# A two-model fp32 block chain on one core: key projection in fp32, low-rank mixes folded into weights, triangular products and attention scores by alternating array halves, splits moved off POOL

## The chip, the cores and the metric

The kernel runs on one core of a Trainium2 chip. The time is device microseconds of one execution. Each engine has its own queue of instructions and runs it in order: PE (TensorE) does the matmuls, DVE (VectorE) and ACT (ScalarE) the elementwise work, POOL (GpSimd) takes some of it, SP (SyncE) starts most DMAs. PE's clock has two levels, 2.4 and 1.2 GHz; the profile gives the granted clock of a stretch as a share of the higher one.

## The reference

All data are float32, 256 positions of width 1024. The chain is RWKV-7 time mixing, a convolutional feed-forward block, sliding-window attention, another such block, then gMLP, MLP, forgetting attention, MLP. Three pieces are touched:

```python
# RWKV time mixing
xx = jnp.pad(x, ((0, 0), (1, 0), (0, 0)))[:, :-1] - x
xr, xw, xk, xv, xa, xg = [x + xx * mu[i] for i in range(6)]
r = xr @ w_rkv[0]; k = xk @ w_rkv[1]; v = xv @ w_rkv[2]
w = -jax.nn.softplus(-(w_decay0 + jnp.tanh(xw @ w_decay1) @ w_decay2)) - 0.5
a = jax.nn.sigmoid(a0 + (xa @ a1) @ a2)
g = jax.nn.sigmoid(xg @ g1) @ g2
def step(S, inp):               # per head, 64 x 64 state, over 256 positions
    r_t, d_t, k_t, v_t, a_t, b_t = inp
    sa = jnp.einsum('bhij,bhj->bhi', S, a_t)
    S = (S * d_t[:, :, None, :] + sa[..., None] * b_t[:, :, None, :]
         + v_t[..., None] * k_t[:, :, None, :])
    return S, jnp.einsum('bhij,bhj->bhi', S, r_t)
# forgetting attention, 16 heads of 64, blocks of 128 queries
logits = jnp.einsum('bhtd,bhsd->bhts', qb, kb) * scale + c_q - c_k   # causal
outs.append(jnp.einsum('bhts,bhsd->bhtd', softmax(logits), vb))
```

## The kernel before

**Weights.** A weight block of 128 x 2048 floats is a *unit*. `fetch` starts its DMA into a raw buffer; `split` turns it into a high part `hi` (a cast, L120, in four pieces, on ACT, some on DVE for units 0 and 1) and a remainder `lo` (raw minus hi, L122, four pieces, on DVE; a table gives some pieces of units 0, 1 and all of 10 to 13 to POOL). `mm3` (L146 to L148) then multiplies hi·hi, hi·lo and lo·hi in three matmuls of the one-pass type fp32r. Inputs of such a product are split the same way. A plain fp32 matmul needs no split; it stands in the trace as two matmul instructions, here called a *pair*.

**RWKV, first part.** For the low-rank branches w and a the kernel makes the mixed inputs x + xx·mu for each of 8 column blocks (`mixk`: one DVE operation L450, or ACT L447 and POOL L448), multiplies them by the 64-column weights (`pw` L474, `pa` L480), and then by the second factor (`pz` L498). For k, r and v `mixsplit` makes the mixed input and splits it (L450, then L138 on ACT and L139 on DVE). Each of the four units of k gives `pk` (48 fp32r matmuls of 128 x 256), its norm (`pn`, `pnb`) and the factors `AR`, `KB`; then come the four units of r (`pr`, L571, L573).

**Triangular products and inversion.** For four chunks c of 64 positions the products of KB and AR of every head go to `pm` (L605): ACT copies KB into a zero-padded tile `KZ` (L601), so that each product contracts over 128 rows of which 64 are zero. DVE masks the result (M, L606). A DVE transpose (L616) begins the inversion of 32 x 32 blocks: 31 steps j of one multiplication into `tm` (L623) and one addition into `TL` (L624), each needing the one before it, then two more transposes (L626, L627). Meanwhile PE runs the projections of v (`pv`), transposes (`pkt`), and the output gate (`pg` L660, L661, then `pgt` L674, L675).

**The chunk loop.** PE makes the blocks of the inverse (`pgm`, `pwm`), then for each chunk `pak`, `ry`, `pu`, `psn`, `py`, each with a copy on DVE or ACT before the next can start. POOL applies the gate (L809 to L813) and scales the state (L788). A group norm (`rv_gn`, L158 and on) and the output projection `wo` follow.

**Forgetting attention.** Scores `plf` (L1004) contract over the 64 rows of a head; heads with even numbers sit in the array's lower, odd ones in its upper 64 rows. Four heads of one half come before four of the other. The products with v (`pof`, L1045) write 64 of 128 output rows by the same rule. PE's queue is filled around them with projections (`fqk`, `fv`, `fg`).

A list scheduler sets each engine's order; the code's order and `tc.high_priority`, `tc.issue_after` steer it.

## Time and profile before

| | us |
|---|---|
| median of 3 runs (lowest, highest) | 1377.25 (1376.43, 1377.95) |
| the profiled execution | 1378.07 |
| its span, first to last instruction | 1376.4 |
| PE busy in the span | 1321.2 |
| DVE busy | 1071.2 |
| ACT busy | 840.4 |
| POOL busy | 129.3 |

An engine's busy time is the time in which one of its instructions runs. An engine idle in a stage that another one bounds costs nothing; so a stage is judged by the engine that is full in it.

### The profile page before, as it was taken

What the parts mean: (1) busy time and instruction counts of PE and PEld (TensorE: products, weight loads), DVE (VectorE), ACT (ScalarE), POOL (GpSimd) and SP (SyncE); (2) the same over time, 40 slices, a digit from 0 to 9 for tenths busy, and PEclk for the clock granted to TensorE, in tenths of its full rate; (3) what the DMA queues carried; (4) which work ended last, traced back from release to release, by engine and by line L of the source; (5) the groups of instructions that cost most, each with busy time, mean ns of one, the idle gap of its engine ahead of it and who ended that gap; (6) DMA issues with size and microseconds to landing.
All of it is one profiled execution on the core that took longest, in us unless ns stands there. A gap on an engine that the chain in (4) does not pass through costs nothing.

```text
span 1376.4 us, 21002 instructions
## 1 busy us (share of the span) xinstructions
PE 1321.2 (96%) x7776; PEld 1125.3 (82%) x7776; DVE 1071.2 (78%) x2296; ACT 840.4 (61%) x1793; POOL 129.3 (9%) x140
## 2 busy tenths in 40 slices
PE   6789888899999999999999999999999999999998
PEld 4788486688888977888888998888887788888887
DVE  8999968799888776998887986766668787576663
ACT  6675444677667874876667854655545766464551
POOL 3366380000000020000001000000000000000000
PEclk9999888999999999999999999999999999999999
DMA  5343202466553523565536554455553644265550
GB/s 212 125 152 111 74 2 92 154 233 226 185 193 128 184 92 107 199 235 202 202 131 225 200 193 158 172 212 191 199 189 118 254 155 151 78 229 192 197 192 31
DMA packets 35111, 226.30 MB, mean 164 GB/s; under 512 B 3744, under 2 KB 6208, under 8 KB 8896
## 3 DMA queue, kind: packets, MB, share of 16 engines
q1 hardware_dynamic: 32496, 215.69, 43.7%
q0 software_dynamic: 1760, 6.30, 1.4%
q10 hardware_dynamic: 752, 2.97, 0.6%
q8 instruction: 61, 1.00, 0.3%
q14 instruction: 42, 0.34, 0.1%
HBM read 223.87 MB, written 1.06 MB: 163 GB/s over the span
## 4 chain that ended last, share of the span: by engine, by line
PE 83%; DVE 12%; ACT 3%; issue 1%; DMA 1%; POOL 1%; DVEq 0%; ACTq 0%; SPq 0%
PE pu L299 9%; PE pm L299 7%; PE pu L297 6%; PE md L148 4%; PE md L146 4%; PE md L147 4%; PE pm L297 4%; PE fd L146 3%; PE fd L147 3%; PE fd L148 3%; DVE lo L122 1%; DVE TL L624 1%; DVE tm L623 1%; PE pu L295 1%; PE gu L148 1%
## 5 line engine op out<-in xcount | busy, mean ns | idle before, releaser
L122 DVE TENSOR_TENSOR lo<-raw,hi 128x512 fp32r<-128x512 f32 x680 | 441.6, 692 | 79.0 <-ACT hi L120 76.9
L120 ACT CAST hi<-raw 128x512 fp32r<-128x512 f32 x696 | 387.5, 618 | 142.8 <-PE md L148 52.3
L299 PE MATMUL pu<-X_n_x,hi 128*128 128x512 f32 x560 | 142.1, 393 | 0.0
L299 PEld LDWEIGHTS pu<-X_n_x,hi 128*128 128x128 f32 x560 | 100.1, 189 | 17.5
L299 PE MATMUL pm<-X_ml_x,hi 128*128 128x512 f32 x392 | 99.7, 393 | 0.0
L297 PEld LDWEIGHTS pu<-X_n_x,lo 128*128 128x128 f32 x640 | 87.4, 190 | 6.2
L297 PE MATMUL pu<-X_n_x,lo 128*128 128x256 f32 x640 | 89.7, 283 | 0.0
L299 PEld LDWEIGHTS pm<-X_ml_x,hi 128*128 128x128 f32 x392 | 70.0, 189 | 12.2
L117 DVE SCALAR_TENSOR_TENSOR lo<-raw,cv,hi 128x256 fp32r<-128x256 f32 (+1 forms) x136 | 67.3, 560 | 14.1 <-ACT hi L116 14.1
L116 ACT ACTIVATE hi<-raw,cv 128x256 fp32r<-128x256 f32 (+1 forms) x136 | 65.9, 560 | 14.5 <-DMA raw<-in_wst 8.9
L305 DVE TENSOR_TENSOR r<-pm,r 128x256 f32<-128x256 f32 x56 | 23.6, 424 | 57.3 <-ACT r L304 57.3
L304 ACT COPY r<-pm 128x256 f32<-128x256 f32 x56 | 20.8, 372 | 74.3 <-PE pm L299 74.3
L297 PEld LDWEIGHTS pm<-X_ml_x,lo 128*128 128x128 f32 x448 | 61.2, 190 | 4.3
L297 PE MATMUL pm<-X_ml_x,lo 128*128 128x256 f32 x448 | 62.7, 282 | 0.0
L939 ACT ACTIVATE ab<-zs,cv 128x256 f32<-128x256 f32 x80 | 47.5, 600 | 16.8 <-DVE zs L305 16.7
L147 PE MATMUL md<-lo,md0h 128*128 128x512 f32 x128 | 49.9, 390 | 0.0
L146 PE MATMUL md<-hi,md0h 128*128 128x512 f32 x128 | 49.8, 389 | 0.0
L148 PE MATMUL md<-hi,md0l 128*128 128x512 f32 x128 | 49.8, 389 | 0.0
L146 PE MATMUL md<-hi,md1h 128*128 128x512 f32 x128 | 49.8, 389 | 0.0
L147 PE MATMUL md<-lo,md1h 128*128 128x512 f32 x128 | 49.8, 389 | 0.0
L148 PE MATMUL md<-hi,md1l 128*128 128x512 f32 x128 | 49.8, 389 | 0.0
L940 DVE SCALAR_TENSOR_TENSOR ab<-zs,cv,ab 128x255 f32<-128x255 f32 x80 | 38.3, 481 | 10.7 <-ACT ab L939 9.2
(558 smaller groups left out, 3352.2 us busy)
## 6 DMA issues: line engine op xcount, KB each, us to landing
raw<-in_wst SPq DMA_DIRECT2D x200, 1024.0 KB, 4.8
g_n<-in_rows POOLq DMA_DIRECT2D x6, 512.0 KB, 4.5
ncb<-cd ACTq DMA_DIRECT2D x2, 1024.0 KB, 9.3
l2a<-in_lora SPq DMA_DIRECT2D x1, 1024.0 KB, 7.4
l2g<-in_lora SPq DMA_DIRECT2D x1, 1024.0 KB, 9.7
g_ml<-in_rows POOLq DMA_DIRECT2D x2, 512.0 KB, 4.1
out<-x SPq DMA_DIRECT2D x4, 256.0 KB, 2.0
cs<-in_cons SPq DMA_DIRECT2D x1, 513.0 KB, 11.9
```

Source lines behind the costliest of these rows:

```text
L116: A.activation(hi[:, q:q + w], r[:, q:q + w], AF.Copy, scale=g[:, j:j + 1])
L117: V.scalar_tensor_tensor(out=lo[:, q:q + w], in0=r[:, q:q + w], scalar=g[:, j:j + 1], in1=hi[:, q:q + w].bitcast(F32), op0=ALU.mult, op1=A ...
L120: (A.copy, V.tensor_copy, G.tensor_copy)[(40 if i < W['vhi'] else 0) // (1, 3, 9, 27)[q // SPL] % 3](hi[:, q:q + SPL], r[:, q:q + SPL])
L122: pe_.tensor_tensor(out=lo[:, q:q + SPL], in0=r[:, q:q + SPL], in1=hi[:, q:q + SPL].bitcast(F32), op=ALU.subtract)
L146: W['mm'].append(PE.matmul(o, lhsT=lh, rhs=rh, start=start, stop=False))
L147: PE.matmul(o, lhsT=lh, rhs=rl, start=False, stop=False)
L148: PE.matmul(o, lhsT=ll, rhs=rh, start=False, stop=stop)
L297: W['mm'].append(PE.matmul(pt[:, 0:T], lhsT=l3[:, k, fs], rhs=X2[:, 0, k, :], start=False, stop=False))
L299: PE.matmul(pt, lhsT=h3[:, k, fs], rhs=X2[:, :, k, :], start=False, stop=k == KD - 1)
L305: V.tensor_tensor(out=out, in0=pt[:, 0:T], in1=out, op=ALU.add)
L939: A.activation(ab[:, s, :], z, AF.Identity, bias=cw(3, fi), scale=cw(2, fi))
L940: V.scalar_tensor_tensor(out=ab[:, s, 1:T], in0=z[:, 0:T - 1], scalar=cw(1, fi), in1=ab[:, s, 1:T], op0=ALU.mult, op1=ALU.add)
```

## The change

The w and a branches use x·W + xx·(mu·W): `l1` holds the weights and a copy scaled by mu on POOL, both branches go through one 128-column product of 16 pairs, and their mixes go away. The four k units are loaded as plain fp32 into the buffers of hi and lo, their input `XK` is mixed but not split, and `pk` is 64 fp32 pairs. No unit before 57 has pieces on POOL, and hi is always cast on ACT; units 10 to 13 are split ahead, at steps 11 and 19 of the inversion, and in the chunk loop. `KZ` goes away: the triangular products contract over 64 rows and alternate between the two halves. `pgt` moves from behind `pg` into the chunk loop. One memset moves from DVE to POOL. In forgetting attention, scores and products with v alternate between heads of both halves, and a square root's table is loaded earlier.

```diff
                 for q in range(0, 2048, SPL):
-                    (A.copy, V.tensor_copy, G.tensor_copy)[(40 if i < W['vhi'] else 0) // (1, 3, 9, 27)[q // SPL] % 3](hi[:, q:q + SPL], r[:, q:q + SPL])
-                    pe_ = G if {0: 8, 1: 8, 10: 15, 11: 15, 12: 15, 13: 15, 57: 12, 58: 12, 59: 12}.get(i, 0) >> q // SPL & 1 else V
+                    A.copy(hi[:, q:q + SPL], r[:, q:q + SPL])
+                    pe_ = G if {57: 12, 58: 12, 59: 12}.get(i, 0) >> q // SPL & 1 else V
                     pe_.tensor_tensor(out=lo[:, q:q + SPL], in0=r[:, q:q + SPL], in1=hi[:, q:q + SPL].bitcast(F32), op=ALU.subtract)
...
         i = W['u']
         W['u'] += 1
-        split(i + (len(W['cyc']) if ahead is None else ahead))
+        split(min(i + (len(W['cyc']) if ahead is None else ahead), W['cap']))
...
-            l1 = wp.tile([P, KD, 128], F32, tag='AR', name='l1')
+            l1 = wp.tile([P, 2, KD, 128], F32, tag='AR', name='l1')
             l2a = wp.tile([P, 2, D], F32, tag='kt', name='l2a')
             l2g = wp.tile([P, 2, D], F32, tag='vt', name='l2g')
-            nc.sync.dma_start(l1, lora1[:, :, 0:128])
+            nc.sync.dma_start(l1[:, 0], lora1[:, :, 0:128])
             nc.sync.dma_start(l2a, lora2[:, 0:2, :])
-            fetch(2)
-            nc.sync.dma_start(cs[:, P:], cons[:, P:])
+            kw = [w0.tile([P, 2048], F32, tag=('hi', 'lo')[u % 2], name=f'kw{u}', bufs=2) for u in range(4)]
+            for u in range(4):
+                nc.sync.dma_start(kw[u], wst[u])
+                if u == 0:
+                    nc.sync.dma_start(cs[:, P:], cons[:, P:])
+            W.update(dma=4, cv=4, u=4, base=4, cap=12)
+            fetch(4 + RAW_B)
+            for i, w in ((1, 0), (4, 1)):
+                sl = slice(w * 64, w * 64 + 64)
+                j = CV['mu'] + i * 8
+                G.tensor_tensor(out=l1[:, 1, :, sl], in0=l1[:, 0, :, sl], in1=cv[:, j:j + 8].unsqueeze(2).to_broadcast([P, KD, 64]), op=ALU.mult)
...
             pw = psum('pw')
             for k in range(KD):
                 V.tensor_tensor(out=xx[:, k], in0=hT[:, k, 0:T], in1=hT[:, k, 1:T + 1], op=ALU.subtract)
-                PE.matmul(pw[0:64, 0:T], lhsT=l1[:, k, 0:64], rhs=mixk(1, k, (V, G)[k % 2]), start=k == 0, stop=k == KD - 1)
+                PE.matmul(pw[:, 0:T], lhsT=l1[:, 0, k, :], rhs=hT[:, k, 1:T + 1], start=k == 0, stop=False)
+            for k in range(KD):
+                PE.matmul(pw[:, 0:T], lhsT=l1[:, 1, k, :], rhs=xx[:, k, :], start=False, stop=k == KD - 1)
             A.activation(gw[0:64, 2, :], pw[0:64, 0:T], AF.Tanh)
-            if W['dma'] < RAW_B:
-                fetch(RAW_B, gate=gw[0:1, 2, 0:1])
-            pa = psum('pa')
-            for k in range(KD):
-                PE.matmul(pa[0:64, 0:T], lhsT=l1[:, k, 64:128], rhs=mixk(4, k, (V, G)[k % 2]), start=k == 0, stop=k == KD - 1)
-            A.copy(gw[0:64, 3, :], pa[0:64, 0:T])
+            A.copy(gw[0:64, 3, :], pw[64:128, 0:T])
...
-            mixsplit(2, 'k')
+            XK = wp.tile([P, KD, T], F32, tag='gt', name='XK')
+            for k in range(KD):
+                mixk(2, k, (V, G)[k % 2], XK[:, k, :])
...
             for u in range(4):
-                pk = proj(f'pk{u}')
+                pk = [psum(f'pk{u}_{f}')[:, 0:T] for f in range(2)]
+                k3 = kw[u].rearrange('p (k c) -> p k c', k=KD)
+                for f in range(2):
+                    for k in range(KD):
+                        PE.matmul(pk[f], lhsT=k3[:, k, f * P:(f + 1) * P], rhs=XK[:, k, :], start=k == 0, stop=k == KD - 1)
...
+            split(10)
             with tc.high_priority():
-                KZ = wp.tile([P, 2, 4, 2, P], F32, tag='av', name='KZ')
-                G.memset(KZ, 0.0)
...
-                            kz = KZ[:, hf]
+                            pms = [psum(f'pm{c}{hf}{e}') for e in range(2)]
+                            for jj in range(4):
+                                for e in range(2):
+                                    es_ = slice(e * 64, e * 64 + 64)
+                                    PE.matmul(pms[e][:, jj * P:(jj + 1) * P], lhsT=KB[es_, hf * 4 + jj, csl], rhs=AR[es_, hf * 4 + jj, csl], start=True, stop=True)
                             for e in range(2):
-                                es_ = slice(e * 64, e * 64 + 64)
-                                A.copy(kz[es_, :, e, :], KB[es_, hf * 4:hf * 4 + 4, csl])
-                            for e in range(2):
-                                pm = psum(f'pm{c}{hf}{e}')
-                                for jj in range(4):
-                                    PE.matmul(pm[:, jj * P:(jj + 1) * P], lhsT=kz[:, jj, e, :], rhs=AR[:, hf * 4 + jj, csl], start=True, stop=True)
-                                lastM = V.tensor_tensor(out=M[:, pc, hf * 8 + e * 4:hf * 8 + e * 4 + 4, :], in0=pm.rearrange('p (i x) -> p i x', i=4), in1=mask.unsqueeze(1).to_broadcast([P, 4, P]), op=ALU.mult)
-                            if c == 2 and hf == 1:
-                                midM = lastM
+                                V.tensor_tensor(out=M[:, pc, hf * 8 + e * 4:hf * 8 + e * 4 + 4, :], in0=pms[e].rearrange('p (i x) -> p i x', i=4), in1=mask.unsqueeze(1).to_broadcast([P, 4, P]), op=ALU.mult)
...
                 for j in range(31):
+                    if j in (11, 19):
+                        split(11 + j // 19)
...
                 for i in range(4):
-                    if 0 != at:
+                    if (3, 3, 5, 5)[i] != at:
                         continue
                     t, hf = (i // 2, i % 2)
-                    pgt = psum(f'pgt{t}{hf}', 'acc')
+                    pgt = psum(f'pgt{t}{hf}')
                     sl = slice(hf * 512, hf * 512 + 512)
                     PE.matmul(pgt, lhsT=gg[:, 0, t * P:(t + 1) * P], rhs=l2g[:, 0, sl], start=True, stop=False)
                     PE.matmul(pgt, lhsT=gg[0:32, 1, t * P:(t + 1) * P], rhs=l2g[0:32, 1, sl], start=False, stop=True)
...
             with tc.issue_after(chain.ins):
-                V.memset(SBt, 0.0)
+                G.memset(SBt, 0.0)
...
+                W.update(cap=NU)
+                if c < 2:
+                    with tc.issue_after(ctx_['s'].ins):
+                        split(13 + c)
...
-            for i0 in range(0, 8, per):
+            for i0 in range(0, 4 * (1 - KZ), per):
+                pls = [psum(f'pl{nm}{n}{hg}{i0}{e}') for e in range(2)]
+                for i in range(per):
+                    for e in range(2):
+                        h = hd(hg, 4 * e + i0 + i)
+                        es_ = slice(e * 64, e * 64 + 64)
+                        PE.matmul(pls[e][:, i * nk:(i + 1) * nk], lhsT=qT[es_, h // 2, n * P:(n + 1) * P], rhs=kT[es_, kidx(h), 0:nk], start=True, stop=True)
+                for e in range(2):
+                    for i in range(per):
+                        s_ = 4 * e + i0 + i
+                        V.tensor_tensor_reduce(out=L[:, s_, 0:nk], in0=pls[e][:, i * nk:(i + 1) * nk], in1=bias(n, hg, s_), scale=1.0, scalar=-3e+38, op0=ALU.add, op1=ALU.max, accum_out=mx[:, s_:s_ + 1])
...
-                    es_ = slice(h % 2 * 64, h % 2 * 64 + 64)
-                    if KZ:
-                        PE.matmul(pl[:, i * nk:(i + 1) * nk], lhsT=qT[:, h // 2, n * P:(n + 1) * P], rhs=kT[:, kidx(h), h % 2, 0:nk], start=True, stop=True)
-                    else:
-                        PE.matmul(pl[:, i * nk:(i + 1) * nk], lhsT=qT[es_, h // 2, n * P:(n + 1) * P], rhs=kT[es_, kidx(h), 0:nk], start=True, stop=True)
+                    PE.matmul(pl[:, i * nk:(i + 1) * nk], lhsT=qT[:, h // 2, n * P:(n + 1) * P], rhs=kT[:, kidx(h), h % 2, 0:nk], start=True, stop=True)
...
+                ss_ = [i0 + i if KZ else (i0 + i) // 2 + 4 * (i % 2) for i in range(per)]
                 for i in range(per):
                     for b in range(n + 1):
-                        PE.transpose(pt[:, i * nk + b * P:i * nk + (b + 1) * P], L[:, i0 + i, b * P:(b + 1) * P], ident)
+                        PE.transpose(pt[:, i * nk + b * P:i * nk + (b + 1) * P], L[:, ss_[i], b * P:(b + 1) * P], ident)
...
-                for i in range(per):
-                    h = hd(hg, i0 + i)
-                    e = h % 2
-                    jj = (i0 + i) % 4
-                    for b in range(n + 1):
+                for i, b in [(i, b) for i in range(per) for b in range(n + 1)] if KZ else [(i, b) for b in range(n + 1) for i in range(per)]:
+                        h = hd(hg, ss_[i])
+                        e, jj = (ss_[i] // 4, ss_[i] % 4)
                         PE.matmul(po[e * 64:e * 64 + 64, jj * P:(jj + 1) * P], lhsT=vv[:, b, vidx(h), :], rhs=PT[:, i * nk + b * P:i * nk + (b + 1) * P], start=b == 0, stop=b == n)
...
             nxt['load']()
+            pre_sqrt(O[1, 1][0][0:1, 3, P - 1:P].bitcast(F32))
             down(lambda u, kk, t: tuple((o[:, (2 * u + kk) % 4, :] for o in O[t, u // 2])), 'wof', res, 3, nxt)
```

First place: POOL and DVE in the inversion. On POOL four units of lo stood between the loading of the group norm's vectors and the memsets of the chunk loop:

```order
L169 DMA g_gn_b<-in_rows 128x1024
L122 TENSOR_TENSOR lo_1405<-raw_1027,hi_1404 128x512 x4
L122 TENSOR_TENSOR lo_1443<-raw_1378,hi_1442 128x512 x4
L122 TENSOR_TENSOR lo_1479<-raw_1414,hi_1478 128x512 x4
L122 TENSOR_TENSOR lo_2280<-raw_1452,hi_2279 128x512 x4
L698 MEMSET Tt 32x32x32 x2
```

Now two of these units (this one and one a few steps before it) stand on DVE between the steps of the inversion:

```order
L634 TENSOR_TENSOR tm_1062<-XDL,TL 128x220
L122 TENSOR_TENSOR lo_1105<-raw_919,hi_1104 128x512
L635 TENSOR_TENSOR TL<-TL,tm_1062 128x22x10
L122 TENSOR_TENSOR lo_1105<-raw_919,hi_1104 128x512
L634 TENSOR_TENSOR tm_1065<-XDL,TL 128x231
L122 TENSOR_TENSOR lo_1105<-raw_919,hi_1104 128x512
L635 TENSOR_TENSOR TL<-TL,tm_1065 128x21x11
L122 TENSOR_TENSOR lo_1105<-raw_919,hi_1104 128x512
```

POOL has nothing left beside the steps; DVE has eight pieces among them (lines 634 and 635 are the old 623 and 624).

Second place: PE behind the inversion. Before, the four `pgt` products stood between `pg` and `pgm`, and `pu` of the first chunk came right behind `pak`:

```order
L674 MATMUL pgt_1599<-l2g,gg 128x512
L675 MATMUL pgt_1599<-l2g,gg 128x512
L693 MATMUL pgm_1606<-XDL,M_1142 32x32 x32
L693 MATMUL pgm_1641<-XDL,M_1205 32x32 x32
L709 MATMUL pwm_1690<-XDL,gm_1604 32x32 x32
L709 MATMUL pwm_1725<-XDL,gm_1605 32x32 x32
L745 MATMUL pak_1772<-UV_1682,M_1142 64x64 x8
L745 MATMUL pak_1784<-UV_1684,M_1142 64x64 x8
L765 MATMUL pu_1794<-RHs,Tt 64x64 x8
```

Now two of them stand between `pak` and `pu`:

```order
L756 MATMUL pak_1508<-UV_1408,M_922 64x64 x8
L685 MATMUL pgt_1566<-l2g,gg 128x512
L686 MATMUL pgt_1566<-l2g,gg 128x512
L685 MATMUL pgt_1570<-l2g,gg 128x512
L686 MATMUL pgt_1570<-l2g,gg 128x512
L776 MATMUL pu_1518<-RHs,Tt 64x64 x8
```

The other two went into the third chunk, among `py`, `psn` and `pak`.

Third place: PE in the scores of forgetting attention, one group of eight heads. Before, four heads of one half, then four of the other:

```order
L148 MATMUL fv_1_11183<-hi_10982,X_mx_x 128x512
L1004 MATMUL plf_11260<-kTf,qTf 128x128 x4
L1004 MATMUL plf_11269<-kTf,qTf 128x128 x4
```

Now the two halves take turns, each with a result tile of its own:

```order
L1017 MATMUL plf_11012<-kTf,qTf 128x128
L1017 MATMUL plf_11013<-kTf,qTf 128x128
L1017 MATMUL plf_11012<-kTf,qTf 128x128
L1017 MATMUL plf_11013<-kTf,qTf 128x128
L1017 MATMUL plf_11012<-kTf,qTf 128x128
```

The number of products is the same.


## Rows read from the trace of the kernel before

**Rows 1.** The page, busy us of each engine, share, instructions.
```profile
PE 1321.2 (96%) x7776; PEld 1125.3 (82%) x7776; DVE 1071.2 (78%) x2296; ACT 840.4 (61%) x1793; POOL 129.3 (9%) x140
```

**Rows 2.** Busy time by stretches: us, each engine, mean granted clock, DMA.
```profile
20.00:118.40 98.40, 85.41 (x646) 80.31 (x647) 93.48 (x178) 68.11 (x145) 47.38 (x44) 0.98 0.28 100
118.40:163.10 44.70, 40.04 (x155) 24.33 (x154) 42.47 (x66) 16.64 (x29) 23.14 (x18) 0.98 0.41 141
163.10:180.00 16.90, 14.19 (x331) 13.60 (x332) 14.08 (x24) 8.06 (x13) 6.69 (x10) 0.55 0.01 3
...
1120.00:1175.00 55.00, 54.97 (x426) 49.39 (x425) 37.74 (x136) 38.07 (x107) 0.00 (x0) 1.00 0.38 135
```

**Rows 3.** VectorE groups, 14 to 104 us: count, busy us, mean ns.
```profile
L122 DVE TENSOR_TENSOR lo<-raw,hi 128x512 fp32r<-128x512 f32 x34 | 27.0, 820 | 0.3 <-ACT hi L120 0.2
L450 DVE SCALAR_TENSOR_TENSOR mix<-HX,cv 128x256 f32<-128x256 f32 x18 | 12.4, 706 | 0.0
L139 DVE TENSOR_TENSOR mx_x<-mix,mx_x 128x256 fp32r<-128x256 f32 x22 | 10.3, 503 | 0.0
```

**Rows 4.** VectorE in order of time (start us, us, what), near 77 us.
```profile
77.19 1.28 DVE L122 TENSOR_TENSOR lo<-raw,hi 128x512 fp32r<-128x512 f32 x2
```

**Rows 5.** PE in order of time, to 50 us.
```profile
24.64 6.39 PE L498 MATMUL pz<-gw,l2a 65*128 65x256 f32 x28 [0.78 <-ACT gw L481]
...
33.01 0.28 PE L146 MATMUL pk<-mx_x,hi 128*128 128x256 f32 x1
33.13 0.28 PE L147 MATMUL pk<-mx_x,hi 128*128 128x256 f32 x1
...
43.08 0.41 PE L147 MATMUL pk<-mx_x,hi 128*128 128x256 f32 x1
```

**Rows 6.** PE in order of time, 100 to 160 us.
```profile
102.78 9.20 PE L605 MATMUL pm<-AR,KZ 128*128 128x128 f32 x80 [0.52 <-DVE pq L573]
...
146.41 0.70 PE L660 MATMUL pg<-xg,l1g 128*128 128x256 f32 x2
147.04 0.62 PE L661 MATMUL pg<-xg,l1g 128*32 128x256 f32 x2
...
156.27 1.13 PE L674 MATMUL pgt<-l2g,gg 128*128 128x512 f32 x2
```

**Rows 7.** VectorE in order of time, the inversion.
```profile
118.39 2.08 DVE L616 STREAM_TRANSPOSE XDL<-XDL 128x1024 f32<-128x1024 f32 x1 [0.45 <-ACT XDL L611]
...
140.39 1.36 DVE L624 TENSOR_TENSOR TL<-TL,tm 128x240 f32<-128x240 f32 x1
141.78 0.42 DVE L623 TENSOR_TENSOR tm<-XDL,TL 128x247 f32<-128x247 f32 x1
...
161.28 1.88 DVE L627 STREAM_TRANSPOSE XDL<-TL 128x1024 f32<-128x1024 f32 x1
```

**Rows 8.** POOL in order of time, the inversion.
```profile
123.45 10.99 POOL L122 TENSOR_TENSOR lo<-raw,hi 128x512 fp32r<-128x512 f32 x8 [3.85 <-ACT hi L120]
...
142.52 4.07 POOL L122 TENSOR_TENSOR lo<-raw,hi 128x512 fp32r<-128x512 f32 x3 [1.04 <-ACT hi L120]
```

**Rows 9.** PE in order of time after the inversion.
```profile
172.77 3.65 PE L745 MATMUL pak<-UV,M 128*64 128x64 f32 x32 [0.32 <-DVE UV L651]
...
182.95 2.03 PE L745 MATMUL pak<-UV,M 128*64 128x64 f32 x32
```

**Rows 10.** VectorE in order of time after the inversion.
```profile
166.07 1.76 DVE L717 MEMSET vc<- 128x2048 f32 x1 [0.21 <-issue]
...
196.99 9.86 DVE L158 TENSOR_SCALAR rv_gn<-vr,epst 128x8 f32<-128x8 f32 x1
```

**Rows 11.** PE in order of time in forgetting attention.
```profile
1121.75 1.71 PE L1004 MATMUL plf<-kTf,qTf 64*128 64x128 f32 x16
1123.39 0.38 PE L146 MATMUL fg<-X_mx_x,hi 128*128 128x256 f32 x1
...
1141.46 1.58 PE L1045 MATMUL pof<-PTf,vvf 128*64 128x128 f32 x16
```

More of the change, by code (lines that the diff above doesn't have):

```diff
@@ L81, in cvc @@
         return cv[:, CV[n] + i:CV[n] + i + 1]
-    W = {'mm': [], 'own': {}, 'late': {}, 'fold': {}, 'gate': 0, 'gap': None, 'rawp': None, 'raw': 0, 'cyc': [], 'lim': 0, 'dma': 0, 'cv': 0, 'u': 0, 'base': 0}
+    W = {'mm': [], 'own': {}, 'late': {}, 'fold': {}, 'gate': 0, 'gap': None, 'rawp': None, 'raw': 0, 'cyc': [], 'lim': 0, 'cap': 0, 'dma': 0, 'cv': 0, 'u': 0, 'base': 0}
     raws, units = ({}, {})
@@ L436, in rwkv, with mixk @@
             m3 = [None]
-            def mixk(i, k, eng=None):
-                if i == 3:
+            def mixk(i, k, eng=None, o=None):
+                if o is not None:
+                    pass
+                elif i == 3:
                     if k % 2 == 0:
@@ L779, in c_s @@
                     if c > 0:
-                        V.tensor_tensor(out=Sn[es_, :, e, :], in0=p3, in1=SE[hf][es_], op=ALU.add)
+                        ctx_['s'] = V.tensor_tensor(out=Sn[es_, :, e, :], in0=p3, in1=SE[hf][es_], op=ALU.add)
                     else:
-                        V.tensor_copy(Sn[es_, :, e, :], p3)
+                        ctx_['s'] = V.tensor_copy(Sn[es_, :, e, :], p3)
                 if c < 2:
@@ L995, in scores @@
             per = 512 // nk
-            for i0 in range(0, 8, per):
+            for i0 in range(0, 4 * (1 - KZ), per):
[9 more added lines that the diff above has]
+                        V.tensor_tensor_reduce(out=L[:, s_, 0:nk], in0=pls[e][:, i * nk:(i + 1) * nk], in1=bias(n, hg, s_), scale=1.0, scalar=-3e+38, op0=ALU.add, op1=ALU.max, accum_out=mx[:, s_:s_ + 1])
+            for i0 in range(0, 8 * KZ, per):
                 pl = psum(f'pl{nm}{n}{hg}{i0}')
@@ L1355, in tile_net @@
     w0 = ctx.enter_context(tc.tile_pool(name='wp0', bufs=1))
-    W.update(rawp=w0, raw=RAW_B, vhi=2)
+    W.update(rawp=w0, raw=RAW_B)
     W.update(cyc=[(w0, 2)] * 2, lim=18)
```

## The prediction

> **What bounds the kernel now.** I read the page first: PE is busy 1321.2 us, 96% of the span [rows 1]. A kernel that full on one engine loses time only where that engine has less to do, or in the stretches where it waits. So I asked next for busy time by stretches. Forgetting attention lies in a stretch where PE has no gap at all (54.97 of 55.00), so a matmul shortened there shortens the kernel. RWKV is different: up to 118.4 us DVE is busy 93.48 of 98.40 us and PE 85.41; in the inversion behind it DVE has 42.47 of 44.70 [rows 2]. There the reader is to see two engines near full, with DVE ahead: what DVE loses is gained only until PE is full. From 163.1 to 180 us neither is full and the granted clock is 0.55 [rows 2]: a chain of small steps, in which every step counts whoever does it.
>
> Then I read each stage in order of time for the price of one instruction, and the mean prices of DVE's groups, which are higher than those of single undisturbed rows: lo has a mean of 0.82 us over its stage, while two pieces in a row take 1.28 [rows 3, 4].
>
> **First part, to the transpose at 118.39.** DVE loses 8 mixes of w and a, 8 subtractions of mixsplit, 8 casts of hi and 14 pieces of lo (units 0 to 3 have 16, two of them were POOL's). At undisturbed rates, 0.42 for the first 24 (the two-input row of 247 columns, [rows 7]) and 0.64 for the pieces [rows 4], that is 10.1 + 9.0 = 19 us. At the stage's means (0.71, 0.50, 0.82; casts taken like subtractions) it is 5.6 + 4.0 + 4.0 + 11.5 = 25 [rows 3]. So DVE alone would let the stage fall by 19 to 25 us.
>
> PE gets in the way. 192 fp32r matmuls go, one every 0.12 us (33.01 to 33.13): 23.0 us. 64 pairs come. The trace has no fp32 product of 128 rows, 128 columns and 256 positions; the nearest is `pz`, 65 rows: 28 instructions or 14 pairs in 6.39 us, 0.456 a pair, hence 29.2 us, or +6.2 [rows 5]. The bounds of this price: nothing below that row, since I see no pair of that width cheaper; above it the gate's first factor, `pg`, where a pair starts 0.63 us before the next (146.41 to 147.04) [rows 6], which makes 40.3 us, or +17.3. I take 0.456, because the shape is that of `pz` in everything but the rows, while `pg` changes its weight tile from 128 to 32 columns at every pair.
>
> That the alternation of tile shapes is what makes `pg` dear is also what the Trainium skill says, in "TensorEngine Tiling (Array Packing)", section "Key Properties": a switch of tiling mode needs the array drained. [...]
>
> The triangular products are 64 pairs at 9.20/40 = 0.23 us [rows 6], 14.7 us. With half the rows, and neighbours in the other half, a pair could lie beside the next, for half of it, 7.4 us; where DVE's masks pace them less is seen. I take 5. PE's floor is then 85.4 + 6.2 - 5 = 86.6 us [rows 2], 11.8 under the 98.4. Some of the 85.4 is only the tail of matmuls in front of a wait (each shows 0.28 us, though the next may start after 0.12 [rows 5]); with the waits gone I take 2 more off. The first part gains **14 us**: PE replaces DVE as its bound. Ends: 3 if pairs cost 0.63, 20 if the halves overlap fully and the tails are larger. The ACT copies into KZ are not counted, since they lie beside the products.
>
> **Inversion.** From 118.39 to the end of the last transpose at 163.16 it is 44.8 us, one chain on DVE [rows 7]. A step of 240 columns takes 1.36 us while POOL subtracts, the next, of 247, 0.42. POOL's pieces run from 123.45 to 146.59, and there are 16 of them [rows 8]; so are the slow steps, one for each piece. The steps grow from 156 to 255 columns there, so the excess is about 0.95 each, 15.2 us. This goes. Eight pieces of lo come in between the steps: 8 x 0.64 = 5.1 us, fully on the chain. Net **-10**; ends -7 (if memsets that now run on POOL slow some steps) and -12.
>
> The Trainium skill names the mechanism, in "SBUF — State Buffer", section "Who interferes with whom": VectorE and GpSimd share a port pair under an exclusive lock, and the loser is blocked fully. The trace agrees, with 1.36 against 0.42.
>
> PE must not become the bound here. It is busy 40.04 us in 44.7 [rows 2], of which `pgt` has 8 pairs or 8.4 us (two instructions show 1.13, one pair each 1.05); 31.6 us remain in a chain of 34.8. It fits, barely. That `pgt` leaves is worth nothing by itself, it was hidden; where it arrives it is not.
>
> **Chunk loop.** Two `pgt` products, 4 pairs, now stand on PE between `pak` and `pu` of the first chunk, where little work hides them. At 1.05 they take 4.2 us; but the clock is low there: 32 instructions of `pak` take 3.65 us, later 2.03 [rows 9], a factor of 1.8, which makes 7.5. Behind them wait `pu`, the copy into UV, `psn` and all chunks after. I take +5.5. The other two in the third chunk lie among its waits for copies: +1.5 of 4.2. Eight pieces of lo in the loop, 5.1 us of DVE, lie in its waits mostly: +1. The memset that goes to POOL took 1.76 of DVE on the way to UV [rows 10]: -1.8. One DVE operation of the group norm took 9.86 us at 196.99 [rows 10] while POOL worked through the gate; POOL's list of gate work is unchanged, so I let it stay. Net **+6**; ends -5 (that block gone for 8, the clock up) and +12.
>
> **Forgetting attention.** Eight pairs of scores, four of each half, take 1.64 us to the next instruction (1121.75 to 1123.39) [rows 11], against 8 x 0.23 = 1.84 at the price of the triangular products: the one change of half gives back nearly a pair. So neighbours in other halves run side by side, and with alternation four of eight could be hidden. There are 32 pairs; the second block's are twice as wide: 2 x 1.64 + 2 x 3.28, less its own switches, about 9. The products with v are 48 pairs at 1.58/8 = 0.20 [rows 11], 9.5 us. Full overlap gives half of 18.5, 9 us; nothing gives 0. I take **-6**: two thirds, as each half's weights are still loaded. Here PE is full, so all of it reaches the end. The early table load lies under PE's work, nothing.
>
> **Sum.** -14 - 10 + 6 - 6 = -24. The profiled execution took 1378.07; 1354 is then its counterpart. The median of runs is 0.8 lower, so I predict **1353**.
>
> **Rivals.**
> - *The fp32 pairs cost more than `pz` shows*, 0.59, half of the way from there to `pg` and more: 64 x 0.59 - 23.0 = +14.8 in place of 6.2, and PE is the bound: 1353 + 8.6 = 1362. For it: no row has this shape. Against: the plain fp32 rows without a change of shape agree, 0.23 for 128 positions and 0.456 for 256 [rows 5, 6].
> - *The chunk loop does not lose*: the gate's POOL work falls at another time and the 9.86 us are gone but for 1 or 2 (-8), and the busier PE before keeps the clock up (-3): 1342. For it: that block depends on what DVE happens to issue while POOL runs. Against: the list of POOL's work is the same.
> - *The alternation is paid for*: each change of half costs what `pg` pays, 0.63 - 0.456 = 0.17, and hides nothing. 80 changes in forgetting attention make +13.6 in place of -6, and in the triangular products 5 are lost: 1353 + 25 = 1378, no change. [...] Against it stands the 1.64.
> - *The alternation does nothing* (the order doesn't hold, or both halves share something): the 6 and 5 are lost: 1364.
> - *Slower*: the clock falls to 1.2 GHz for k and r. A matmul of k shows 0.41 in place of 0.28 at 43.08 [rows 5], so this level occurs in this stage. k and r take 29.2 + 23.0 = 52 us of PE, at the factor 1.8 another 42: 1353 + 42 = 1395. It decides from 24/42, 57% of the stage at the low level. Against: the low stretch came behind waits, and the change has fewer.
>
> **How the numbers follow.** The forecast, with 1345 to 1361 as its own range, has 0.5; dear pairs 0.13; the better loop 0.15; alternation without effect 0.1; paid for 0.05; the slow clock 0.04; the rest 0.03 lies outside on either side. From 1338 to 1368 no more than 2 in 10 is left out. A measurement of this kernel tells some 0.2%, 2.8 us, from no change. Faster: all but paid alternation, the slow clock and part of the rest, 0.91; same 0.04; slower 0.05.
>
> **What the profile after would show.** Pairs of `pk` every 0.44 to 0.46 us; the transpose that begins the inversion near 104 us; the inversion's steps all at 0.2 to 0.43 us and 34 to 35 us from that transpose to the end of the last; `pu` of the first chunk 4 to 7 us later behind `pak` than before; eight pairs of scores in about 1.0 us. The prediction is wrong if the transpose comes after 110 us, if slow steps remain in the inversion, if the loop grows by over 12 us, or if the eight pairs still take 1.6.

## The result, and the profile after

The changed kernel takes 1361.91 us, the median of four runs from 1357.66 to 1367.48, against 1376.96 for the kernel before (four runs, 1376.43 to 1377.95). The ratio is 0.9892, 95% interval 0.9856 to 0.9929: faster by 1.1%, or 15 us. The forecast was 24 us. The profiled execution took 1361.48, its span 1359.7. Its page, busy time of each engine, against [rows 1]:

```profile
PE 1316.6 (97%) x7712; PEld 1120.3 (82%) x7712; DVE 1040.7 (77%) x2273; ACT 820.9 (60%) x1754; POOL 100.9 (7%) x116
```

DVE lost 30.5 us and POOL 28.4, PE only 4.6. What of it reached the end is read stage by stage, from one landmark to the next in both traces (first `fqk`: the first projection of forgetting attention; the stage ends with the first weight load of the MLP behind it; the chunk loop ends where the last `wo` starts):

| stage, us | before | after | moved | forecast |
|---|---|---|---|---|
| start to the transpose that begins the inversion | 118.4 | 113.4 | -5.0 | -14 |
| inversion, to the end of the last transpose | 44.8 | 35.3 | -9.4 | -10 |
| chunk loop, to the last `wo` | 82.3 | 85.0 | +2.7 | +6 |
| middle models | 813.2 | 811.6 | -1.6 | 0 |
| forgetting attention | 153.7 | 150.5 | -3.2 | -6 |

The sum, -16.5, is but for 0.1 the difference of the two profiled executions (1378.07 to 1361.48). The inversion came as forecast. The first part gave a third of what was expected, and most of the miss lies there. So I cut it again: where `pk` begins behind `pz` (in the changed kernel four of its 128 instructions ran ahead of `pz`), at the first `pr` and at the start of the last `pr`. The view is busy time by stretches of the kernel after (us, then PE, PE's loads, DVE, ACT, POOL, the granted clock, DMA); below these four stand a piece of the third, and one around the start of the inversion:

```profile
20.00:28.04 8.04, 7.71 (x35) 6.13 (x35) 6.53 (x13) 6.29 (x15) 3.11 (x4) 1.00 1.04 405
28.04:60.70 32.66, 31.58 (x165) 27.49 (x163) 21.65 (x49) 17.90 (x39) 9.72 (x8) 1.00 0.17 64
60.70:95.00 34.30, 30.75 (x242) 29.89 (x241) 27.02 (x49) 15.75 (x35) 14.01 (x17) 0.95 0.34 123
95.00:113.40 18.40, 14.68 (x126) 12.15 (x126) 17.19 (x28) 7.41 (x13) 6.71 (x6) 0.89 0.08 21
...
65.00:70.00 5.00, 2.20 (x14) 2.00 (x13) 4.93 (x7) 2.48 (x6) 5.00 (x8) 0.83 0.60 203
...
110.00:115.00 5.00, 5.00 (x16) 4.32 (x17) 3.79 (x6) 1.23 (x2) 1.59 (x4) 0.50 0.61 211
```

The same four stretches in the kernel before:

```profile
20.00:30.68 10.68, 9.25 (x41) 6.79 (x41) 10.68 (x21) 6.60 (x18) 5.31 (x7) 1.00 0.06 25
30.68:66.40 35.72, 29.46 (x226) 28.45 (x225) 34.60 (x67) 22.63 (x50) 15.03 (x12) 0.95 0.32 118
66.40:101.10 34.70, 30.43 (x249) 29.44 (x248) 32.53 (x62) 24.20 (x53) 20.99 (x19) 1.00 0.40 143
101.10:118.40 17.30, 16.27 (x137) 15.62 (x136) 15.67 (x31) 14.67 (x26) 6.06 (x7) 1.00 0.05 21
```

So 2.6 us are won ahead of `pk`, 3.1 in k and 0.4 in r, and 1.1 are lost behind the last `pr`. In k DVE is relieved by 13.0 us, and PE is nearly full, as planned: it waits 5.2 us less (6.26 to 1.08) and works 2.1 more. In r DVE is relieved by 5.5, PE has about the same work, and the stretch falls only by 0.4. From 65 to 70 us PE is busy 2.20 of 5.00 and POOL all of it.

What happens there, POOL first, in order of time:

```profile
61.89 1.75 POOL L597 TENSOR_TENSOR xg<-xg,HX 128x256 f32<-128x256 f32 x2 [1.13 <-ACT xg L596]
63.60 1.74 POOL L574 TENSOR_TENSOR KB<-kt,EE 128x512 f32<-128x512 f32 x1
65.30 3.91 POOL L597 TENSOR_TENSOR xg<-xg,HX 128x256 f32<-128x256 f32 x5
69.17 3.17 POOL L459 TENSOR_TENSOR mix<-mix,HX 128x256 f32<-128x256 f32 x4
72.31 1.19 POOL L597 TENSOR_TENSOR xg<-xg,HX 128x256 f32<-128x256 f32 x1
73.46 1.27 POOL L575 TENSOR_TENSOR kkr<-kkr,av 128x512 f32<-128x512 f32 x1
```

DVE in the same stretch, the norm of the last unit of k:

```profile
64.22 1.67 DVE L122 TENSOR_TENSOR lo<-raw,hi 128x512 fp32r<-128x512 f32 x1
65.81 0.68 DVE L562 TENSOR_TENSOR vn<-vn,nr 128x8 f32<-128x8 f32 x1
66.53 0.65 DVE L563 TENSOR_TENSOR vn<-vn,nr 128x8 f32<-128x8 f32 x1
67.21 0.56 DVE L564 SCALAR_TENSOR_TENSOR nr<-vn,nr 128x8 f32<-128x8 f32 x1
67.69 2.59 DVE L461 SCALAR_TENSOR_TENSOR mix<-HX,cv 128x256 f32<-128x256 f32 x3
```

And PE, the product that waits for that norm:

```profile
68.53 1.12 PE L570 MATMUL pnb<-cs,nb 128*128 128x128 f32 x4 [2.80 <-ACT nb L566]
```

POOL works without a gap from 61.89 to 74.73, first on `xg`, the input of the output gate, whose first product on PE starts at 138.2. Three DVE operations of 8 columns take 0.56 to 0.68 us in that time, and a piece of lo 1.67 in place of 0.64 [rows 4]. `nb`, which ACT makes from their result, is late, and PE, in order, stands behind it with `pr` in its queue.

In the inversion, against [rows 7], VectorE in order of time:

```profile
113.39 2.00 DVE L625 STREAM_TRANSPOSE XDL<-XDL 128x1024 f32<-128x1024 f32 x1 [1.21 <-ACT XDL L620]
...
120.18 0.69 DVE L122 TENSOR_TENSOR lo<-raw,hi 128x512 fp32r<-128x512 f32 x1 [2.20 <-ACT hi L120]
...
129.25 0.41 DVE L634 TENSOR_TENSOR tm<-XDL,TL 128x240 f32<-128x240 f32 x1
...
130.13 0.42 DVE L634 TENSOR_TENSOR tm<-XDL,TL 128x247 f32<-128x247 f32 x1
...
146.80 1.94 DVE L638 STREAM_TRANSPOSE XDL<-TL 128x1024 f32<-128x1024 f32 x1
```

The step of 240 columns took 1.36 and takes 0.41; no slow step is left. A wait is new: 2.20 us for ACT's cast `hi` of the first unit that is split between the steps.

In the chunk loop, against [rows 9], PE in order of time:

```profile
156.71 3.65 PE L756 MATMUL pak<-UV,M 128*64 128x64 f32 x32
160.29 1.22 PE L685 MATMUL pgt<-l2g,gg 128*128 128x512 f32 x2
161.44 1.12 PE L686 MATMUL pgt<-l2g,gg 32*128 32x512 f32 x2
162.49 1.12 PE L685 MATMUL pgt<-l2g,gg 128*128 128x512 f32 x2
163.54 1.12 PE L686 MATMUL pgt<-l2g,gg 32*128 32x512 f32 x2
164.59 2.08 PE L776 MATMUL pu<-RHs,Tt 128*64 128x64 f32 x32
```

`pgt` takes 4.30 us, with the clock high again (0.98 in these 4.30 us, 0.50 in the `pak` before them): about 1.05 a pair, the undisturbed price, and not 1.8 times as much.

Forgetting attention, against [rows 11]: PE in order of time, a group of scores in the first block with what follows it, and the second block:

```profile
1108.27 1.16 PE L1017 MATMUL plf<-kTf,qTf 64*128 64x128 f32 x16
1109.36 0.39 PE L146 MATMUL fg<-X_mx_x,hi 128*128 128x256 f32 x1
...
1122.33 1.56 PE L1017 MATMUL plf<-kTf,qTf 64*128 64x256 f32 x10
1124.42 1.13 PE L1017 MATMUL plf<-kTf,qTf 64*128 64x256 f32 x6 [0.53 <-ACT gate L1352]
1126.42 1.95 PE L1060 MATMUL ptrf<-cs,b 128*128 128x128 f32 x8 [0.87 <-DVE mxf L1021]
...
1130.08 2.00 PE L1017 MATMUL plf<-kTf,qTf 64*128 64x256 f32 x16
...
1145.58 1.63 PE L1066 MATMUL pof<-PTf,vvf 128*64 128x128 f32 x24
1147.14 0.44 PE L1060 MATMUL ptrf<-cs,ncb 128*128 128x128 f32 x2
```

Eight pairs take 1.09 us to the next instruction, where they took 1.64. The products with v: 12 pairs from 1145.58 to 1147.14, 0.13 a pair, before 8 pairs in 1.58, 0.20 [rows 11]. But PE, full there before [rows 2], now waits for the gate and for the maximum `mxf`.

### The profile page after: what moved, and what is told of

Read it like the earlier page. It is cut to its first block, busy times and chain, and to the rows that moved or that the text cites. A ratio compares the mean times of both kernels' runs of the same rounds, so it can differ in the third digit from the quotient of the medians.

```text
span 1359.7 us, 20766 instructions
## 1 busy us (share of the span) xinstructions
PE 1316.6 (97%) x7712; PEld 1120.3 (82%) x7712; DVE 1040.7 (77%) x2273; ACT 820.9 (60%) x1754; POOL 100.9 (7%) x116
## 4 chain that ended last, share of the span: by engine, by line
PE 80%; DVE 11%; ACT 3%; DMA 2%; issue 2%; POOL 1%; ACTq 0%; DVEq 0%
PE pu L299 9%; PE pm L299 7%; PE pu L297 6%; PE md L146 4%; PE md L147 4%; PE md L148 4%; PE pm L297 4%; PE fd L146 3%; PE fd L148 3%; PE fd L147 3%; DVE lo L122 2%; DMA raw<-in_wst 2%; PE pk L541 2%; PE pu L295 1%; PE gu L148 1%
## 5 line engine op out<-in xcount | busy, mean ns | idle before, releaser
L120 ACT CAST hi<-raw 128x512 fp32r<-128x512 f32 x688 | 383.0, 618 | 151.7 <-PE md L148 54.9
L954 ACT ACTIVATE ab<-zs,cv 128x256 f32<-128x256 f32 x80 | 47.4, 600 | 17.6 <-DVE zs L305 17.5
```

The source lines that it names most:

```text
L120: A.copy(hi[:, q:q + SPL], r[:, q:q + SPL])
L954: A.activation(ab[:, s, :], z, AF.Identity, bias=cw(3, fi), scale=cw(2, fi))
```

## The experiments

All kernels compute the whole output. Changes of 1 or 2 us are near what the runs can tell; each interval is given.

**e0: the same kernel again.**

> The changed kernel once more, timed beside the experiments, because its four times spread from 1357.7 to 1367.5 us while the kernel before spreads by 1.5. Theory A, the clock: the spread is time at the lower granted clock, so the mean granted clock of each run falls as its time rises, by about 0.001 for each 1.2 to 1.4 us. Theory B, something that the clock doesn't show (a DMA that lands late): times differ at equal clock. Either way a median of 1358 to 1365 us.

Measured: 1360.8 (1359.54 to 1364.83), ratio 0.989 [0.9876, 0.9905]. The result repeats. The run of 1364.83 had a mean granted clock of 0.984, the other four 0.986 to 0.987; in the four runs first shown, 0.989 goes with 1357.66, 0.986 with 1361.48 and 1362.34, and 0.981 with 1367.48. So the spread of this kernel goes with the clock, some 1.2 us for each 0.001 (9.8 us over 0.008; at equal clock runs still differ by up to 2.8).

**e1: the gate's input later.** One copy on POOL makes `xg` wait for the second unit of r:

```diff
+            G.tensor_copy(xg[0:1, :, 0], AR[0:1, 2, 0:8])
             with tc.issue_after(xga.ins):
                 for k in range(KD):
                     A.activation(xg
```

> The gate's mixed input xg is computed on ACT and POOL only once the second unit of r is there, and so no longer beside the last unit of k; nothing else changes. Theory A: the first part gained 5 us in place of 14 because POOL works without a gap from 61.9 to 74.7 us, slows the DVE steps of the last unit of k, and makes PE wait 2.8 us and then run short of input: the transpose that begins the inversion comes 4 to 6 us earlier, at 107 to 109 us, and the kernel is 4 to 6 us faster. Theory B, the price: PE's own work with the plain fp32 pairs fills this part, and the transpose stays within 1 us of 113.4.

Measured: 1355.59 (1355.03 to 1359.44), ratio 0.9854 [0.9839, 0.9869], 5.2 us under e0. The transpose comes at 109.2, and r takes 31.1 us in place of 34.3. VectorE at the same place, in order of time:

```profile
65.09 0.15 DVE L562 TENSOR_TENSOR vn<-vn,nr 128x8 f32<-128x8 f32 x1
65.28 0.17 DVE L563 TENSOR_TENSOR vn<-vn,nr 128x8 f32<-128x8 f32 x1
65.48 0.17 DVE L564 SCALAR_TENSOR_TENSOR nr<-vn,nr 128x8 f32<-128x8 f32 x1
65.56 1.27 DVE L461 SCALAR_TENSOR_TENSOR mix<-HX,cv 128x256 f32<-128x256 f32 x3
```

The three small operations take 0.15 to 0.17, the mixes 0.42 in place of 0.86, and PE's wait for `nb` falls from 2.80 to 0.90. So the queue of POOL, not DVE's sum of work, held this place. The edit moves ACT's part of `xg` too (eight operations of 0.49 us), and what that is worth wasn't separated.

**e2: k split as before, all else changed.**

```diff
-            kw = [w0.tile([P, 2048], F32, ... for u in range(4)]
+            fetch(2)
...
-                mixk(2, k, (V, G)[k % 2], XK[:, k, :])
+            mixsplit(2, 'k')
...
-                        PE.matmul(pk[f], lhsT=k3[:, k, ...], rhs=XK[:, k, :], ...)
+                pk = proj(f'pk{u}')
```

> Only the key projection is undone: k is again a product of split fp32r parts, with its splits on DVE, ACT and POOL; the folded low-rank branches and all else stay as changed. Theory A (plain fp32 pairs at 0.43 us cost PE 6 us and free DVE of 15): the transpose comes 4 to 8 us later, at 117 to 121, and the kernel is slower by as much. Theory B (the folding of the low-rank branches gave most of the 5 us, and fp32 for k is a wash): within 2 us of the changed kernel.

Measured: 1361.68, ratio 0.9896 [0.9882, 0.991], 0.9 above e0, inside both intervals; the transpose at 115.1. By itself k in fp32 is worth about 1 us, hardly to be told from nothing.

**e10: both, k split and the gate's input later** (the edits of e1 and e2).

> The key projection undone and the gate's mixed input late, together. Undoing k alone cost 0.9 us, and the late input alone gained 5. Theory A: plain fp32 for k was worth nothing because the wait behind the last unit of k swallowed what it freed on DVE; with the wait gone it shows, and this kernel is 4 to 8 us slower than the one with the late input alone, 1360 to 1363 us. Theory B: PE's 6 us more and DVE's relief cancel whatever comes behind: 1355 to 1358 us.

Measured: 1361.8 (1360.34 to 1362.52), ratio 0.9884 [0.987, 0.9898], 6.2 above e1; the transpose at 116.5 against e1's 109.2. So delaying `xg` gives nothing with k split, and k in fp32 gives 6 us with `xg` delayed. The rows of e1 fit this reading: the fp32 product makes room on DVE, and `xg` on POOL filled it.

**e12: the kernel before with the folded low-rank weights alone.** Edit: the hunks on `l1` and `pw` of the change, nothing else.

> The kernel before with the folded low-rank branches alone. Theory A: they bring the second factor (pz) 2 us forward and take 8 DVE mixes out of a stage that DVE bounds, 3 to 5 us before the transpose, and this is all that the first part of the changed kernel gained (5 us, since undoing fp32 for k cost it 1): 1372 to 1374 us. Theory B: the folding is swallowed by the wait behind the last unit of k as well, and the 5 us came only from all edits together: 1376 us or more.

Measured: 1371.92 (1370.67 to 1373.39), ratio 0.9961 [0.9948, 0.9974], -4.9. The transpose comes at 113.3, the place it has in the changed kernel; the inversion still takes 44.8.

**e4: the kernel before with DVE in place of POOL for units 10 to 13, nothing else.**

```diff
-{0: 8, 1: 8, 10: 15, 11: 15, 12: 15, 13: 15, 57: 12, 58: 12, 59: 12}
+{0: 8, 1: 8, 57: 12, 58: 12, 59: 12}
```

> The kernel before with one part of the change alone: the pieces of lo of units 10 to 13 are subtracted on DVE, none on POOL. Theory A (POOL's subtractions hold DVE back, one slow step of 1.36 us for each piece): no slow step is left, the sixteen pieces cost 16 x 0.64 = 10 us if all lie between the steps, so the inversion takes 39 to 41 us in place of 44.8, less if some lie behind it, and the kernel is 4 to 9 us faster than before. Theory B (the steps of 156 to 255 columns are slow in themselves or for PE's reads): the slow steps remain, and the kernel is 5 to 10 us slower.

Measured: 1368.87 (1367.95 to 1371.25), ratio 0.9938 [0.9923, 0.9953], -8.2. The inversion takes 37.0 us, against 44.8. VectorE in order of time, to be held against [rows 7]:

```profile
133.25 0.68 DVE L122 TENSOR_TENSOR lo<-raw,hi 128x512 fp32r<-128x512 f32 x1
133.85 0.40 DVE L624 TENSOR_TENSOR TL<-TL,tm 128x240 f32<-128x240 f32 x1
134.29 0.42 DVE L623 TENSOR_TENSOR tm<-XDL,TL 128x247 f32<-128x247 f32 x1
```

Twice as many pieces of lo stand on the chain as in the changed kernel, and it is still 8 us shorter: POOL's pieces cost the steps more than the same pieces cost on DVE. At its end PE is 2.9 us late: `pgm` begins at 159.7, the last transpose ends at 156.8.

**e5: `pgt` back behind `pg`,** all else changed.

```diff
-                    if (3, 3, 5, 5)[i] != at:
+                    if 0 != at:
...
-                    pgt = psum(f'pgt{t}{hf}')
+                    pgt = psum(f'pgt{t}{hf}', 'acc')
```

> The changed kernel with the gate's second product (four matmul groups, 8.4 us) back in its old place between the gate's first factor and the blocks of the inverse. Theory A: in the changed kernel PE is done only just before the last transpose (it waits 1.3 us there), so 8.4 us more delay the chunk loop by about 7, of which 4 to 5 come back in the loop: 2 to 4 us slower than the changed kernel. Theory B: the old place was as good, since the loop pays 4.3 us behind the first chunk's first step at full price: 0 to 2 us faster.

Measured: 1360.41 (1356.65 to 1364.2), ratio 0.9875 [0.9853, 0.9898]; its interval and e0's overlap. PE is 5.7 us late at `pgm`, and from the last transpose to the last `wo` it takes 85.1 us against 85.0.

**e13: the same in a kernel with the gate's input later and KB scaled on ACT** (the edits of e1, e5 and the first of e11).

> The changed kernel with the gate's input late, KB's scaling on ACT, and the gate's second product in its old place; the order in forgetting attention as changed. The old place of the second product was worth 0 to 1 us in the changed kernel. Theory A: PE starts the projection of v earlier here, by 5 us, so it gets through the second product before the last transpose and the loop is 5 us shorter: 1350 to 1352 us. Theory B: PE's start and the transpose move together, and the two places are a wash again: 1354 to 1356 us.

Measured: 1355.7 (1354.57 to 1363.11), ratio 0.9855 [0.9835, 0.9875]; e11, where `pgt` stands in the loop, has 0.9834 [0.982, 0.9847]. PE is 5.8 us late. Within these intervals either place costs the same.

**e3: forgetting attention as before,** scores and products with v in the old order, all else changed.

```diff
-            for i0 in range(0, 4 * (1 - KZ), per):
+            for i0 in range(0, 0, per):
...
-            for i0 in range(0, 8 * KZ, per):
+            for i0 in range(0, 8, per):
...
-                ss_ = [i0 + i if KZ else (i0 + i) // 2 + 4 * (i % 2) for i in range(per)]
+                ss_ = [i0 + i for i in range(per)]
...
```

> Forgetting attention alone goes back to four heads of one half and then four of the other, in scores and in the products with v. Theory A: alternation saved PE 6 us there, of which 3 were given back in a new wait behind the first group of the second block's scores and a low clock after it: this kernel is 3 us slower than the changed one, the wait of 0.5 and 0.9 us near 1124 us is gone, and 8 pairs of scores take 1.6 us in place of 1.1. Theory B: the wait is there with either order (it came from an earlier arrival): this kernel is 6 us slower.

Measured: 1366.51 (1363.33 to 1375.43), ratio 0.9939 [0.9918, 0.9961], 5.7 above e0. PE in order of time, against the rows of the second block above:

```profile
1130.95 2.96 PE L1030 MATMUL plf<-kTf,qTf 64*128 64x256 f32 x16
...
1137.21 2.56 PE L1070 MATMUL pof<-PTf,vvf 128*64 128x128 f32 x16 [1.65 <-ACT PTf L1066]
...
1156.10 2.45 PE L1070 MATMUL pof<-PTf,vvf 128*64 128x128 f32 x24
```

The wide group takes 2.96 where the alternating one took 2.00, 12 pairs of products with v 2.45 in place of 1.63. A wait (1.65) stands here in the old order too, with a granted clock of 0.76 from 1135 to 1140 and 0.90 in the 5 us behind that. The kernel before has neither: its stage takes 153.7 us, e3's 157.1 in this profile, which is of its longest run.

**e8: only the products with v alternate** (the first two edits of e3).

> The changed kernel with only the scores of forgetting attention back in the order four and four; the products with v still alternate. Theory A: scores gave 2 us of the 6 (0.55 for each of two groups of eight pairs, 0.9 for one of the second block, nothing for the one behind which PE waits), so it is 1 to 3 us slower than the changed kernel. Theory B: alternating scores need two result banks at once and so brought the wait for the gate's copy on ACT, which ate what they saved: within 1 us or faster.

Measured: 1364.53 (1361.73 to 1364.87), ratio 0.9906 [0.9892, 0.9919]; e0 has 0.989. By the ratios the scores are worth 2.2 us of the 6 (0.0016 x 1377), by the medians 3.7; the intervals overlap, so only their rough share is told.

**e6: the triangular products without turns,** on 64 rows still.

```diff
-                            for jj in range(4):
-                                for e in range(2):
+                            for e in range(2):
+                                for jj in range(4):
```

> The changed kernel with the triangular products, still of 64 rows, in the order four of one half, then four of the other. Theory A: DVE's masks bound that stretch (16 of 0.6 us and six other operations in 16 us), so the order of PE's products moves the transpose by less than 1 us, and the 5 us that the prediction took for it were never to be had: 1360 to 1362 us. Theory B: alternation shortens it: 2 to 5 us slower.

Measured: 1361.77 (1357.89 to 1371.5), ratio 0.99 [0.9873, 0.9927], 1.4 above e0 by the ratios (0.001 x 1377), inside both intervals. From the last `pr` to the transpose it takes 18.0 us, with turns 18.4, though PE's granted clock is 0.75 there, with turns 0.89; DVE is busy 17.21 of the 18.0. The masks set the pace, and how PE makes their input is worth next to nothing.

**e11: the best version.** `xg` later as in e1; KB scaled on ACT in place of POOL; and another order of the work that fills PE's queue in forgetting attention:

```diff
-                            G.tensor_tensor(out=KB[:, :, csl], in0=KB[:, :, csl], in1=EC[:, :, c:c + 1].to_broadcast([P, KD, P]), op=ALU.mult)
+                            for j in range(KD):
+                                A.activation(KB[:, j, csl], KB[:, j, csl], AF.Copy, scale=EC[:, j, c:c + 1])
...
-'s00 a0 s01 b0 g1 s10 p00 s11 g2 g3 p10 p01 p11'
+'s00 a0 s01 b0 a1 s10 b1 p00 s11 g2 g3 p10 p01 p11'
```

> The changed kernel with three edits: the gate's mixed input late; the scaling of KB between the triangular products on ACT (24 operations of 128 columns) in place of POOL (three of 1.91 us); and in forgetting attention half of one gate projection placed behind the first scores of the second block. Theory A (POOL's three operations slow three DVE operations there by 0.8 to 1.4 us each, and the wait behind those scores is PE's for want of other work): 2 to 3 us before the transpose and 1 to 3 us in forgetting attention, 1350 to 1353 us. Theory B (ACT's operations are then in the way of its own copies, or the order does not matter): 1355 us or more.

Measured: 1354.67 (1353.78 to 1355.68), ratio 0.9834 [0.982, 0.9847], 1.7% under the kernel before and 0.9 us under e1 (the two intervals overlap); the 1350 to 1353 of its first theory didn't come. The transpose comes at 107.9. VectorE in order of time, three operations that POOL's KB had slowed to 1.18, 1.27 and 2.03 in the changed kernel:

```profile
96.23 0.42 DVE L139 TENSOR_TENSOR mx_x<-mix,mx_x 128x256 fp32r<-128x256 f32 x1
...
97.76 0.42 DVE L139 TENSOR_TENSOR mx_x<-mix,mx_x 128x256 fp32r<-128x256 f32 x1
...
101.08 0.69 DVE L122 TENSOR_TENSOR lo<-raw,hi 128x512 fp32r<-128x512 f32 x1
```

From the last `pr` to the transpose it takes 15.5 us, against 18.4 in the changed kernel and 17.6 in e1. The new order in forgetting attention gave nothing: 150.6 us against 151.0 in e1, with waits for the gate (0.91) and `mxf` (0.35) still there.

## Why it was right, and where not

**The sign and the wide range, 1338 to 1368, held; the narrow one, 1345 to 1361, was missed by 0.9 us, and the size was 9 us short.** The step that failed is "The first part gains 14 us: PE replaces DVE as its bound." By a sign that the prediction itself named, a transpose after 110 us, it is wrong there: the transpose came at 113.4 (114.2 in e0). That the total isn't further off is partly luck: the first part fell 9 us short and forgetting attention 3, while the chunk loop lost 3 less than forecast. And 1362 is also what the rival of dear pairs gave, so the time alone would have spoken for a wrong cause.

The price of k was right. A pair of `pk` takes 0.435 us (28 instructions from 28.04 to 34.13), a shade under the 0.456 taken. The stage's PE work is 84.72 us, near the floor of 86.6 less 2 for tails, but by two errors that cancel: in k it grew by 2.1 where 6.2 was taken, behind the last `pr` it fell by 1.6 where 5 was taken. What was wrong was the step from busy time to length: I let the stretch shrink to PE's work, as if PE would then be full. PE stayed idle 8.7 us of it. The four stretches show where: in k PE is idle for only 1.08 us; in r (3.55) and behind it (3.72) it waited for a chain that runs over POOL. POOL had 47.4 us of work in this part, and I counted only what DVE lost. I hadn't asked whom POOL slows, nor when its work would fall. e1 shows the one place (-5.2), e11 the other (17.6 to 15.5 us from the last `pr` to the transpose, though the time fell only by 0.9); with both the transpose is at 107.9 (109.0 in e13, which has both too), 4 to 5 us behind the 104 that the prediction named.

Nor were the 5 us of the triangular products there to be had, since DVE's masks pace them (e6). I had named that doubt and taken 5 all the same.

**Inversion: right, in cause and size.** -9.4 of -10. e4 shows the cause by itself. The Trainium skill says in "SBUF — State Buffer", section "Who interferes with whom", that VectorE and GpSimd share a port pair under a lock; the traces agree, with 1.36 against 0.41 for the same step and, in the first part, 0.68 against 0.15 for the same 8 columns. All of this was in view: I used the rule for the inversion, and for nothing ahead of it.

**Chunk loop: +2.7 of +6.** The term was too large because the 1.8 for a low clock didn't apply: `pgt` took 4.30, not 7.5. `pu` comes 7.9 us behind the first `pak`, before 4.2: 3.7 later, where 4 to 7 were forecast. The 9.86 us block of DVE [rows 10] is gone; in its place stand several of 1 to 2 us, of which the first is this one, VectorE in order of time:

```profile
190.99 1.80 DVE L158 TENSOR_SCALAR rv_gn<-vr,epst 128x8 f32<-128x8 f32 x2
...
196.06 1.72 DVE L836 TENSOR_TENSOR yt<-yt,grs 128x512 f32<-128x512 f32 x1
```

In the whole loop PE is idle 8.0 us, before 12.9: a wait of 10.0 for `yt`, which stood behind that block, is down to 0.6, but one of 4.9 for `vc` is new. And PE is busy 77.0 us, before 69.4, that is 7.6 more, about what `pgt` takes. The loss isn't only the price of `pgt`'s new place: with `pgt` back in the old one e5 takes 85.1 us here as well, with PE 5.7 late, and e13 86.3, with PE 5.8 late. e4, where `pgt` never moved, has 83.6, so about half of the loss, with PE 2.9 late. The account that fits, though no run isolates it: where the inversion is 8 or 9 us shorter, the product no longer fits beside it, and is paid on one side of `pgm` or the other. I wrote "it fits, barely", which was for PE without `pgt`; that holds, and the sentence that leaving "is worth nothing by itself" doesn't.

**Forgetting attention: -5.7 by the experiment, -3.2 in the pair of profiles.** Eight pairs took 1.09 us, forecast 1.0. e3 gives 5.7 us for both orders together, with a wait and a lower clock on either side. In the pair of profiles only the changed kernel has them: PE's work in the stage fell by 4.8 us, from 152.5 to 147.7, though it now holds a granted clock of 0.66 from 1125 to 1130, and its idle time rose by 1.6, the new waits in the second block (0.53 and 0.87 above). The 2 to 3 us between the two figures lie there. A wait stands there in e3 too, with the old order (1.65), so the alternation isn't what makes PE wait; e11's attempt to cover the waits failed. What makes PE run dry there stays open.

**The rivals.** Dear fp32 pairs: refuted by 0.435. The loop that doesn't lose: its half, the block that dissolves, came true, and its gain went into the new wait and PE's added work. Alternation paid for: refuted. At 0.17 for each of 80 changes of half, forgetting attention would have lost 13.6 us; it won 3 to 6. By the Trainium skill's "TensorEngine Tiling (Array Packing)", section "Key Properties", a change of tiling mode, not one of the tile alone, drains the array. The trace agrees: eight pairs that change between the two halves of one mode take 1.09 us, not more than the 1.64 of four and four. Alternation without effect: refuted in forgetting attention, true in the triangular products. A slow clock in k and r: it occurs, though not in the runs near the median, as far as their mean clock (0.986) tells. In the profiled runs of e3 and e6 PE's first stretch shows it, busy time by stretches of e6:

```profile
20.00:40.00 20.00, 18.75 (x56) 14.96 (x55) 14.48 (x34) 14.06 (x30) 4.38 (x6) 0.66 0.55 214
```

The changed kernel's own profile has 1.00 there. These two runs reach the first `pr` at 68.9 and 68.8 us, 8 later than the 60.7 above. What decides it from run to run wasn't found; the kernel before spreads by 4.4 us in the 12 runs beside e0 to e3 (1374.60 to 1378.96), this one by 9.8.

**The parts don't add up.** Folding -4.9 and POOL's pieces -8.2, each alone in the kernel before, and attention -5.7, k -0.9 and turns about -1, each taken out of the changed kernel, make -21; together they give -15. Some 2 to 3 of the rest are the new waits and the low clock in forgetting attention, which the -5.7 doesn't hold. Two more places where parts meet are seen: the shorter inversion has less room for PE's work, and k and `xg` stand in each other's way (e2, e10). I can't split the 6 us further.

## What to carry to other kernels

Before the busy time taken off one engine is counted as time, walk every engine of the stage in order of time, the nearly idle one too: here POOL, at 7% of the span, decided by its place whether 17 to 21 us of relief on VectorE ahead of the transpose (e2 against the changed kernel, e10 against e1) were worth 1 us or 6. Work with a late consumer should be tied to a late start, not left to fill the first gap that it finds. And price an edit with its neighbours: an edit that gives nothing may be waiting for another one.
